# Per-row factors and second key copies of a two-layer fp32 trunk by transfers instead of transpositions

## The chip, the cores and the metric

One core of one Trainium2 chip runs the kernel. The metric is the device time of one execution in microseconds; it is the median of 3 runs. The engines are called PE (matmul), PEld (its weight load), DVE (vector), ACT (scalar), POOL (the general engine) and SP (which issues transfers); a q behind a name is the engine's sequencer.

## What is computed

A trunk of two layers on a sequence of 512 tokens of 1024 features, all in fp32. Layer 0 mixes by attention, layer 1 by a state-space scan (ssd); each is followed by a gated feed-forward part (ffn). Every part begins with an RMS norm and ends with a residual sum.

```python
for layer in range(DEPTH):
    h = rmsnorm(x, norm_mix[layer])
    if layer % 2 == 0: mix = attn_layer(h, ...)
    else:              mix = ssm_layer(h, ...)
    x = x + mix
    h = rmsnorm(x, norm_ffn[layer])
    x = x + conv_ffn(h, ...)
```

The attention layer has 8 heads B (a band of 3 chunks of 64 tokens, 2 key heads for 8 query heads, sinks) and 8 heads A (all earlier chunks, learned bias by relative position), each of 64 features, queries and keys normalised by head. A head's output is divided by its sum of exponentials:

```python
e = jnp.exp(sc - m)
p = e / (jnp.sum(e, axis=-1, keepdims=True) + jnp.exp(snk - m))
```

The ssd layer norms its gated output again in four groups of 512 features: `yg * rsqrt(mean(yg * yg) + EPS)`.

## The kernel before

Activations lie with features on the 128 partitions and the 512 tokens along the free axis, so x is eight tiles X[0] to X[7] of 128x512. A fp32 product is made of two rounded parts, hi and lo, of each operand: three matmuls (hi hi, lo hi, hi lo) in `mm3` (L154 to L159) and in `project` (L335 to L352, the input projection of attention, tokens on partitions). Weights are loaded by SP into wr, cast to wh by ACT (L150), and the rest wl is made by DVE (L151). PSUM has four banks mm for dense products, three ax for transpositions and scores, one po for head outputs.

The program sets the order within limits; a scheduler then lays each engine's instructions in one queue, which the engine goes through in order. `weave` mixes the attention units with dense products. The work the change touches:

- `Sq.rstd` (L199) makes 1/rms of each token as a 128x4 column block, tokens on partitions. The rest of the kernel needs it along the free axis, equal on all partitions: `rows` (L208 to L214) transposes four broadcast columns on PE (L211) and ACT copies the 128x512 result R to SBUF (L213). It is called seven times: for the first ffn (R is read by L627 and L637), for the ssd layer (`v` L734, the early tiles L705, `normalise` L685 to L689), four times in `gated` (R is read by `out_part`, L897, whose product is added to X in `accumulate`, L251), and for the second ffn.
- `totals` (L379 to L398), once per head pair, eight times: the reciprocals of the sums `rec` (128x8) are widened by two ACT copies (L391), transposed on PE (L395) and copied by ACT (L397) to R. `finish_pair` (L400) multiplies the head output in po by R on DVE (L402) and splits it (L405, L406).
- Scores (`scores`, L364 and L365 on PE) are evicted by DVE (L367) with the bias and go through ACT (L368); `flip` transposes them (L374, L376), `pv` multiplies with the values (L413).
- Two query heads of a pair lie on one 128-partition tile each with the other half empty, so a key head is needed in both halves. DVE writes each normalised key head twice (`twice`, L553; queries are scaled in L558), and `keys` (L321 to L333) transposes each head's 128 columns (L327), ACT makes hi (L329) and DVE lo (L330). There are ten key heads in three blocks: 2, 4 and 4.
- POOL makes the bias tiles of heads B (L451), fills a corner of each bias tile of heads A after SP has loaded it (L471), and six sums of squares (L195). Transfers from the scratch `scr` in DRAM, broadcast over the partitions, are issued by SP in the scan (L794).

Of the kernel before, what the change touches and what calls it, by code (L numbers as in the profile page):

```python
# [15 lines left out]
F32 = mybir.dt.float32  # L16
# [45 lines left out]
def trunk(ctx: ExitStack, tc: tile.TileContext, xin, w_ai, w_av, w_ao_b, w_ao_a, relp, w_dt, w_si, w_so,  # L62
# [116 lines left out]

    class Sq:  # L180
# [27 lines left out]
        def rows(self, r):  # L208
            bp = axps()
            for t in range(NT):  # L210
                nc.tensor.transpose(bp[:, t * P:(t + 1) * P], r[:, t:t + 1].to_broadcast([P, P]), ident)  # L211
            R = slot()
            nc.scalar.copy(R, bp)  # L213
            return R  # L214

# [58 lines left out]
    def attention(op, nxt, first):  # L274
# [46 lines left out]
        def keys(kn, n, g):  # L321

            hi, lo = [], []
            for h in range(n):
                tp = axps()
                for t in range(NT):
                    nc.tensor.transpose(tp[:, t * P:(t + 1) * P], kn[t][:, h * P:(h + 1) * P], ident)  # L327
                kh, kl = slot(F32R), slot(F32R)
                nc.scalar.activation(kh, tp, AF.Copy, scale=g)  # L329
                nc.vector.scalar_tensor_tensor(kl, tp, g, kh.bitcast(F32), ALU.mult, ALU.subtract)  # L330
                hi.append(kh)
                lo.append(kl)
            return hi, lo  # L333
# [45 lines left out]
        def totals(st, sink):  # L379
# [9 lines left out]
            wide = dslot()  # L389
            for i in range(2):  # L390
                nc.scalar.copy(wide.rearrange("q (p i d) -> q p i d", p=NT, i=2)[:, :, i, :],  # L391
                               rec[:, i * NT:(i + 1) * NT].unsqueeze(2).to_broadcast([P, NT, 64]))
            bp = axps()
            for p in range(NT):
                nc.tensor.transpose(bp[:, p * P:(p + 1) * P], wide[:, p * P:(p + 1) * P], ident)  # L395
            R = dslot()
            nc.scalar.copy(R, bp)  # L397
            return R  # L398

        def finish_pair(po, R):  # L400
            t = dslot()
            nc.vector.tensor_tensor(t, po, R, ALU.mult)  # L402
# [93 lines left out]
        def parts(grps):  # L496
# [9 lines left out]
            for grp, (nh, nv, turns) in enumerate(grps):  # L506
# [36 lines left out]
                twice = [None] * NT  # L543
                if nh:
                    f = head_scales(ss, nh)
                    nk = sum(n for _, name, _, n, _ in turns if name == "k")
                    nq = nh - nk
                    for t in range(NT):
                        w = raw[t][:, :nh * 64].rearrange("p (h d) -> p h d", h=nh)
                        ft = f[:, nh * t:nh * t + nh].unsqueeze(2)  # L550
                        if nk:
                            twice[t] = cslot()
                            nc.vector.tensor_tensor(  # L553
# [52 lines left out]
    def ffn(layer, op, nxt):  # L606
# [10 lines left out]
        def in_tile(f):  # L617
# [6 lines left out]
            if f == 0:  # L624
                R = op.sq.rows(r)
# [447 lines left out]
```

## Time and profile before

| | before |
|---|---|
| median of 3 runs | 1331.98 us (1331.82 to 1333.86) |
| profiled execution | 1335.82 us |
| its span on the engines | 1334.0 us |
| PE, PEld busy | 1323.0, 1076.1 us |
| DVE, ACT, POOL busy | 897.2, 592.8, 20.5 us |
| bytes moved | 130.73 MB, 98 GB/s |
| granted TensorE clock, mean | 0.997 |

Busy time of an engine is the time in which at least one of its instructions ran; matmuls overlap in the pipeline, so one's duration is longer than the distance to the next. A chain of waits is followed back from the last instruction to what released each step. A timeline line has the start, the duration, the engine, the line of the program, the operation with what it writes and reads, how many were merged into it, and in brackets how long the engine was idle before it and what ended that.

### The profile page before, as it was taken

How to read it: one execution, taken by the hardware profiler on the slowest of the kernel's cores; microseconds unless marked ns; L12 is line 12 of the kernel's file. 1: busy time of each engine (PE TensorE's matmuls, PEld its weight loads, DVE VectorE, ACT ScalarE, POOL GpSimd, SP SyncE). 2: the span in 40 equal slices, each digit the busy share in tenths (PEclk: the TensorE clock that was granted, in tenths of full speed). 3: DMA queues.
4: the chain of work that ended last, by engine and by line, in shares of the span. 5: the costliest groups of instructions: out<-in, count | busy, mean ns of one | idle time of the engine just before them, and what ended most of it. 6: DMA issues, size and time to landing. Idle time of an engine off the chain costs nothing.

```text
span 1334.0 us, 17143 instructions
## 1 busy us (share of the span) xinstructions
PE 1323.0 (99%) x6576; PEld 1076.1 (81%) x6576; DVE 897.2 (67%) x1494; ACT 592.8 (44%) x1042; POOL 20.5 (2%) x26
## 2 busy tenths in 40 slices
PE   9999999999999999999999999999999999999998
PEld 7777877788888888887788887887888888888887
DVE  5676565876446646458988896898986644664642
ACT  6576655533223323244655645546443322332321
POOL 0000000000000000020000000000000000000000
PEclk8999999999999999999999999999999999999999
DMA  7112241233332333232443333332333333333322
GB/s 238 64 52 66 74 155 44 87 99 99 103 95 95 95 96 97 85 105 62 144 127 111 103 103 96 112 99 91 95 95 95 96 99 101 100 95 95 96 72 86
DMA packets 42561, 130.73 MB, mean 98 GB/s; under 512 B 4848, under 2 KB 6128, under 8 KB 42480
## 3 DMA queue, kind: packets, MB, share of 16 engines
q1 hardware_dynamic: 41760, 129.12, 31.2%
q8 instruction: 52, 0.85, 0.3%
q10 hardware_dynamic: 720, 0.52, 0.2%
q14 instruction: 29, 0.24, 0.1%
HBM read 127.46 MB, written 2.16 MB: 97 GB/s over the span
## 4 chain that ended last, share of the span: by engine, by line
PE 93%; DVE 4%; ACT 2%; DMA 1%; issue 1%; ACTq 0%; SPq 0%; POOL 0%; POOLq 0%; DVEq 0%
PE mm L159 77%; PE mm L348 7%; PE po L413 2%; PE po L847 1%; PE ax L374 1%; DVE wl L151 1%; PE po L852 1%; PE ax L835 1%; PE ax L364 1%; ACT wh L150 1%; PE ax L365 1%; PE ax L804 1%; DMA c<-in_xin 0%; DVE d L685 0%; PE ax L201 0%
## 5 line engine op out<-in xcount | busy, mean ns | idle before, releaser
L159 PE MATMUL mm<-s,wh 128*128 128x512 f32 x3148 | 766.7, 391 | 0.7 <-DVE s L251 0.5
L159 PEld LDWEIGHTS mm<-s,wh 128*128 128x128 f32 x3148 | 585.1, 188 | 125.7 <-issue 4.6
L150 ACT CAST wh<-wr 128x1024 fp32r<-128x1024 f32 (+2 forms) x222 | 226.9, 1022 | 443.4 <-PE mm L159 404.7
L159 PE MATMUL mm<-s,wl 128*128 128x512 f32 x1574 | 398.1, 390 | 0.0
L159 PEld LDWEIGHTS mm<-s,wl 128*128 128x128 f32 x1574 | 293.8, 188 | 61.6 <-issue 1.5
L151 DVE TENSOR_TENSOR wl<-wr,wh 128x1024 fp32r<-128x1024 f32 (+2 forms) x222 | 262.8, 1184 | 41.7 <-ACT wh L150 41.1
L251 DVE TENSOR_TENSOR s<-s,mm 128x512 f32<-128x512 f32 x64 | 43.6, 687 | 125.6 <-PE mm L159 123.4
L348 PE MATMUL mm<-wh,s 128*128 128x512 f32 (+1 forms) x320 | 99.9, 389 | 3.0 <-ACT s L162 1.3
L627 DVE TENSOR_TENSOR d<-mm,s 128x512 f32<-128x512 f32 x44 | 30.4, 691 | 93.3 <-PE mm L159 90.5
L348 PEld LDWEIGHTS mm<-wh,s 128*128 128x128 f32 x320 | 58.3, 193 | 15.2 <-issue 2.4
L631 DVE SCALAR_TENSOR_TENSOR d<-d,pt,d 128x511 f32<-128x511 f32 x88 | 65.9, 749 | 3.8 <-ACT d L629 2.4
L634 ACT ACTIVATE d<-d 128x512 f32<-128x512 f32 x44 | 27.9, 634 | 86.1 <-DVE d L631 86.1
L348 PE MATMUL mm<-wl,s 128*128 128x512 f32 (+1 forms) x160 | 61.5, 384 | 0.0
L635 DVE SCALAR_TENSOR_TENSOR d<-d,d 128x512 f32<-128x512 f32 x44 | 30.5, 692 | 30.4 <-ACT d L634 30.4
L712 DVE SCALAR_TENSOR_TENSOR s<-mm,pt,s 128x511 f32<-128x511 f32 (+2 forms) x57 | 42.5, 745 | 9.6 <-ACT s L710 9.3
L813 ACT ACTIVATE c<-c,acs 128x128 f32<-128x128 f32 x128 | 41.8, 399 | 0.0
L368 ACT ACTIVATE c<-c,sm 128x256 f32<-128x256 f32 (+3 forms) x64 | 33.4, 526 | 16.5 <-DVE sm L367 15.2
L629 ACT ACTIVATE d<-d,pt 128x512 f32<-128x512 f32 x44 | 35.8, 814 | 6.0 <-DVE d L627 6.0
L637 DVE TENSOR_TENSOR d<-mm,s 128x512 f32<-128x512 f32 x44 | 30.4, 691 | 8.6 <-PE mm L159 8.5
L641 ACT CAST s<-d 128x512 fp32r<-128x512 f32 x44 | 27.4, 623 | 18.5 <-DVE d L638 18.5
L348 PEld LDWEIGHTS mm<-wl,s 128*128 128x128 f32 x160 | 31.1, 194 | 4.7 <-issue 0.3
L638 DVE TENSOR_TENSOR d<-d,d 128x512 f32<-128x512 f32 x44 | 30.5, 692 | 1.4
(155 smaller groups left out, 1026.1 us busy)
## 6 DMA issues: line engine op xcount, KB each, us to landing
wr<-in_w_fi SPq DMA_DIRECT2D x88, 512.0 KB, 3.6
wr<-in_w_si SPq DMA_DIRECT2D x40, 512.0 KB, 3.6
wr<-in_w_fo_a SPq DMA_DIRECT2D x32, 512.0 KB, 3.6
c<-scr SPq DMA_DIRECT2D x32, 256.0 KB, 4.1
wr<-in_w_so SPq DMA_DIRECT2D x16, 512.0 KB, 3.6
wr<-in_w_ai SPq DMA_DIRECT2D x12, 512.0 KB, 3.6
wr<-in_w_fo_b SPq DMA_DIRECT2D x16, 384.0 KB, 3.0
wr<-in_w_ai SPq DMA_DIRECT2D x8, 256.0 KB, 5.1
```

The lines of the kernel that those rows point to most:

```text
L150: nc.scalar.copy(h[:, cs], raw[:, cs])
L151: nc.vector.tensor_tensor(lo[:, cs], raw[:, cs], h[:, cs].bitcast(F32), ALU.subtract)
L159: nc.tensor.matmul(dst, a, b, start=start and i == 0, stop=stop and i == n - 1)
L251: nc.vector.tensor_tensor(X[m], X[m], acc, ALU.add)
L348: nc.tensor.matmul(us[t], a, b, start=k == 0 and i == 0, stop=k == KD - 1 and i == 2)
L368: nc.scalar.activation(e, e, AF.Exp, bias=st[:, n:n + 1], scale=-1.0, accum_out=st[:, 8 + n:9 + n])
L629: nc.scalar.activation(c, g, AF.Identity, bias=col(cw + 4 * f + 3), scale=col(cw + 4 * f + 2))
L631: nc.vector.scalar_tensor_tensor(c[:, sh:], g[:, :S - sh], col(cw + 4 * f + j), c[:, sh:], ALU.mult, ALU.add)
L635: nc.vector.scalar_tensor_tensor(c, th, 1.0, c, ALU.add, ALU.mult)
L638: nc.vector.tensor_tensor(u, u, c, ALU.mult)
L712: nc.vector.scalar_tensor_tensor(c[:, sh:], g[:, :S - sh], col(w0 + 3 - sh), c[:, sh:], ALU.mult, ALU.add)
L813: nc.scalar.activation(t[:, i * P:(i + 1) * P], bc[hf][:, i * P:(i + 1) * P], AF.Relu, bias=acs[:, hs + i:hs + i + 1], scale=-1.0)
```

## The change

A new function `spread` takes a block of columns (tokens on partitions) to PE for one transposition, has ACT copy the few rows that come out to SBUF, stores them from there in DRAM by a transfer that ACT issues, and loads them, broadcast over the partitions, by a transfer that POOL issues. `rows` and `totals` call it in place of their transpositions. `finish_pair` has ACT copy po to SBUF at once; DVE multiplies that copy. `keys` transposes two key heads at a time, and three half transfers issued by POOL make from each hi and lo tile the two doubled ones: first both halves of the new tile k from the second half of x, then the second half of x from its first. The scaling by 1/rms of a head is one DVE product per tile for queries and keys.

```diff
--- before.py
+++ after.py
@@ -177,6 +177,17 @@
             nc.vector.scalar_tensor_tensor(y, t, 1.5, y, ALU.add, ALU.mult)
         return y
 
+    def spread(vals, n, dst, ap):
+
+        tp = axps()[:n, :P]
+        nc.tensor.transpose(tp, vals, ident)
+        flat = sm.tile([8, P], F32, tag="flat", bufs=2, name=nm("flat"))
+        nc.scalar.copy(flat[:n, :], tp)
+        row = dp.tile([8, P], F32, name=nm("row"))
+        nc.scalar.dma_start(row[:n, :], flat[:n, :])
+        nc.gpsimd.dma_start(dst, bass.AP(tensor=row.tensor, offset=row.offset, ap=ap))
+        return dst
+
     class Sq:
 
 
@@ -206,12 +217,7 @@
             return rsqrt(v, NT)
 
         def rows(self, r):
-            bp = axps()
-            for t in range(NT):
-                nc.tensor.transpose(bp[:, t * P:(t + 1) * P], r[:, t:t + 1].to_broadcast([P, P]), ident)
-            R = slot()
-            nc.scalar.copy(R, bp)
-            return R
+            return spread(r, NT, slot(), [[0, P], [1, S]])
 
     class Operand:
 
@@ -318,18 +324,25 @@
                     res.append(q)
             return res
 
-        def keys(kn, n, g):
+        def move(dst, i, src, j):
+            nc.gpsimd.dma_start(dst[HALF[i], :].bitcast(F32), src[HALF[j], :].bitcast(F32))
+
+        def keys(kn, c0, n, g):
 
             hi, lo = [], []
-            for h in range(n):
+            for b in range(n // 2):
                 tp = axps()
                 for t in range(NT):
-                    nc.tensor.transpose(tp[:, t * P:(t + 1) * P], kn[t][:, h * P:(h + 1) * P], ident)
-                kh, kl = slot(F32R), slot(F32R)
-                nc.scalar.activation(kh, tp, AF.Copy, scale=g)
-                nc.vector.scalar_tensor_tensor(kl, tp, g, kh.bitcast(F32), ALU.mult, ALU.subtract)
-                hi.append(kh)
-                lo.append(kl)
+                    nc.tensor.transpose(tp[:, t * P:(t + 1) * P], kn[t][:, c0 + b * P:c0 + (b + 1) * P], ident)
+                h, l = slot(F32R), slot(F32R)
+                nc.scalar.activation(h, tp, AF.Copy, scale=g)
+                nc.vector.scalar_tensor_tensor(l, tp, g, h.bitcast(F32), ALU.mult, ALU.subtract)
+                for res, x in ((hi, h), (lo, l)):
+                    k = slot(F32R)
+                    move(k, 0, x, 1)
+                    move(k, 1, x, 1)
+                    move(x, 1, x, 0)
+                    res += [x, k]
             return hi, lo
 
         def project(wsrc, width, evict, mid):
@@ -386,20 +399,12 @@
                 nc.vector.tensor_tensor(st[:, 8:16], st[:, 8:16], x, ALU.add)
             rec = small(8)
             nc.vector.reciprocal(rec, st[:, 8:16])
-            wide = dslot()
-            for i in range(2):
-                nc.scalar.copy(wide.rearrange("q (p i d) -> q p i d", p=NT, i=2)[:, :, i, :],
-                               rec[:, i * NT:(i + 1) * NT].unsqueeze(2).to_broadcast([P, NT, 64]))
-            bp = axps()
-            for p in range(NT):
-                nc.tensor.transpose(bp[:, p * P:(p + 1) * P], wide[:, p * P:(p + 1) * P], ident)
-            R = dslot()
-            nc.scalar.copy(R, bp)
-            return R
+            return spread(rec, 8, dslot(), [[S, 2], [0, 64], [1, S]])
 
         def finish_pair(po, R):
             t = dslot()
-            nc.vector.tensor_tensor(t, po, R, ALU.mult)
+            nc.scalar.copy(t, po)
+            nc.vector.tensor_tensor(t, t, R, ALU.mult)
             h = slot(F32R)
             lo = slot(F32R)
             nc.scalar.copy(h, t)
@@ -540,32 +545,21 @@
                 if nv and grp == 0:
                     for t in range(NT):
                         v_copy(t, raw[t][:, nh * 64:])
-                twice = [None] * NT
                 if nh:
                     f = head_scales(ss, nh)
-                    nk = sum(n for _, name, _, n, _ in turns if name == "k")
-                    nq = nh - nk
                     for t in range(NT):
                         w = raw[t][:, :nh * 64].rearrange("p (h d) -> p h d", h=nh)
-                        ft = f[:, nh * t:nh * t + nh].unsqueeze(2)
-                        if nk:
-                            twice[t] = cslot()
-                            nc.vector.tensor_tensor(
-                                twice[t][:, :nk * P].rearrange("p (h e d) -> p h e d", h=nk, e=2),
-                                w[:, nq:, :].unsqueeze(2).to_broadcast([P, nk, 2, 64]),
-                                ft[:, nq:, :].unsqueeze(3).to_broadcast([P, nk, 2, 64]), ALU.mult)
-                        if nq:
-                            nc.vector.tensor_tensor(w[:, :nq, :], w[:, :nq, :], ft[:, :nq, :].to_broadcast([P, nq, 64]),
-                                                    ALU.mult)
-
-                def turn(raw=raw, twice=twice, vs=vs, nv=nv, turns=turns):
+                        nc.vector.tensor_tensor(w, w, f[:, nh * t:nh * t + nh].unsqueeze(2).to_broadcast([P, nh, 64]),
+                                                ALU.mult)
+
+                def turn(raw=raw, vs=vs, nv=nv, turns=turns):
                     for res, name, c0, n, g in turns:
                         if name == "v":
                             res["v"] = v_tiles(vs, nv)
                         elif name == "q":
                             res["q"] = queries(raw, c0, g)
                         else:
-                            res["k"] = keys(twice, n, g)
+                            res["k"] = keys(raw, c0, n, g)
 
                 if nh:
                     late[0] = turn
@@ -619,10 +613,8 @@
             gate = dense(w_fi[layer, f, 0])
             if f == 0:
                 op.squares()
-                r = op.sq.rstd(1024)
+                R = op.sq.rows(op.sq.rstd(1024))
             up = dense(w_fi[layer, f, 1])
-            if f == 0:
-                R = op.sq.rows(r)
             g = dslot()
             nc.vector.tensor_tensor(g, gate, R, ALU.mult)
             c = dslot()
```

The new line numbers: `spread` has its transposition on L183, the copy on L185, the store on L187, the load on L188; the moves are L328; the scores are L377 and L378.

The scheduler moves other instructions too. On DVE, at the start of the ssd layer, before (L734 makes `v`, L705 the first tile, L712 its convolution, L685 and L689 the normalised tiles):

```order
L151 TENSOR_TENSOR wl_5485<-wr_5483,wh_5484 128x1024
L734 TENSOR_TENSOR v<-mm_5197,s_5266 32x128 x4
L705 TENSOR_TENSOR d_5279<-mm_5236,s_5266 128x512
L742 TENSOR_SCALAR v<-v,pt 128x128
L712 SCALAR_TENSOR_TENSOR s_5281<-d_5279,pt,s_5281 128x511
L745 TENSOR_SCALAR ta<-ta 128x128
L712 SCALAR_TENSOR_TENSOR s_5281<-d_5279,pt,s_5281 128x510
L746 RECIPROCAL ta<-ta 128x128
L712 SCALAR_TENSOR_TENSOR s_5281<-d_5279,pt,s_5281 128x509
```

and now, where they are L726, L697, L704, and L734 the step that was L742:

```order
L151 TENSOR_TENSOR wl_5454<-wr_5452,wh_5453 128x1024
L726 TENSOR_TENSOR v<-mm_5165,s_5229 32x128 x4
L697 TENSOR_TENSOR d_5248<-mm_5204,s_5229 128x512
L734 TENSOR_SCALAR v<-v,pt 128x128
L151 TENSOR_TENSOR wl_5504<-wr_5502,wh_5503 128x1024
L704 SCALAR_TENSOR_TENSOR s_5250<-d_5248,pt,s_5250 128x511
L737 TENSOR_SCALAR ta<-ta 128x128
L704 SCALAR_TENSOR_TENSOR s_5250<-d_5248,pt,s_5250 128x510
```

The reader of R still stands right behind the split of a weight, and everything behind it in the queue follows in nearly the same order, with one split moved up into it.

On DVE, at the end of the ssd layer, before (L897 multiplies by R, here s_8414, L251 adds to X, L166 makes lo for the ffn):

```order
L151 TENSOR_TENSOR wl_8595<-wr_8593,wh_8594 128x1024
L897 TENSOR_TENSOR d_8473<-mm_8460,s_8414 128x512
L251 TENSOR_TENSOR s_1980<-s_1980,d_8473 128x512
L897 TENSOR_TENSOR d_8492<-mm_8479,s_8414 128x512
L251 TENSOR_TENSOR s_1982<-s_1982,d_8492 128x512
L151 TENSOR_TENSOR wl_8650<-wr_8648,wh_8649 128x1024
L166 SCALAR_TENSOR_TENSOR s_8477<-s_1980,pt,s_8476 128x512
L897 TENSOR_TENSOR d_8518<-mm_8505,s_8414 128x512
```

and now (L889 multiplies by R, here s_8381, L257 adds):

```order
L151 TENSOR_TENSOR wl_8568<-wr_8566,wh_8567 128x1024
L151 TENSOR_TENSOR wl_8623<-wr_8621,wh_8622 128x1024
L889 TENSOR_TENSOR d_8446<-mm_8433,s_8381 128x512
L889 TENSOR_TENSOR d_8465<-mm_8452,s_8381 128x512
L257 TENSOR_TENSOR s_1948<-s_1948,d_8446 128x512
L257 TENSOR_TENSOR s_1950<-s_1950,d_8465 128x512
L889 TENSOR_TENSOR d_8491<-mm_8478,s_8381 128x512
L889 TENSOR_TENSOR d_8511<-mm_8498,s_8381 128x512
L166 SCALAR_TENSOR_TENSOR s_8450<-s_1948,pt,s_8449 128x512
```

One more split stands ahead of the first product with R, and products and sums come in pairs; a further split that stood between them has gone behind.

On POOL, in the middle of attention, where heads B end and the keys of heads A begin, the change has (L188 loads R of a pair, L328 moves keys, L456 and L476 are the former L451 and L471):

```order
L456 TENSOR_SCALAR c_1067<-dist 128x256
L456 TENSOR_SCALAR c_1075<-dist 128x256
L188 DMA d_1111<-row_1116 128x1x512
L476 MEMSET c_1391 64x64
L188 DMA d_1321<-row_1326 128x1x512
L328 DMA s_1350<-s_1346 64x512 x2
L328 DMA s_1354<-s_1347 64x512 x2
L328 DMA s_1367<-s_1363 64x512
L328 DMA s_1346<-s_1346 64x512
L328 DMA s_1367<-s_1363 64x512
```

where before there was only

```order
L451 TENSOR_SCALAR c_1078<-dist 128x256
L451 TENSOR_SCALAR c_1086<-dist 128x256
L471 MEMSET c_1410 64x64
L471 MEMSET c_1419 64x64
L471 MEMSET c_1580 64x64
L471 MEMSET c_1589 64x64
```

The transfers now stand in the queue between products that wait for buffers and a MEMSET that waits for the load of its tile.

## Rows read from the trace of the kernel before

**Rows 1.** Page, busy time, share and instructions of each engine; the chain of waits by engine

```profile
PE 1323.0 (99%) x6576; PEld 1076.1 (81%) x6576; DVE 897.2 (67%) x1494; ACT 592.8 (44%) x1042; POOL 20.5 (2%) x26
...
PE 93%; DVE 4%; ACT 2%; DMA 1%; issue 1%; ACTq 0%; SPq 0%; POOL 0%; POOLq 0%; DVEq 0%
```

**Rows 2.** Groups by line: out<-in, shapes, count | busy us, mean ns | idle before

```profile
L327 PE MATMUL ax<-ident,c 128*128 128x128 f32 x40 | 6.2, 276 | 0.4 <-DVE c L553 0.4
...
L395 PE MATMUL ax<-ident,d 128*128 128x128 f32 x32 | 4.9, 275 | 0.5 <-DVE sm L367 0.5
...
L211 PE MATMUL ax<-ident,sm 128*128 128x128 f32 x28 | 4.3, 275 | 0.7 <-DVE sm L177 0.6
...
L213 ACT COPY s<-ax 128x512 f32<-128x512 f32 x7 | 4.1, 586 | 16.7 <-PE ax L211 16.7
```

**Rows 3.** Timeline around a head pair's sums: start, us, engine, line, operation

```profile
208.20 0.60 PE L395 MATMUL ax<-ident,d 128*128 128x128 f32 x4
...
208.56 0.36 PE L364 MATMUL ax<-s,s 128*128 128x256 f32 x1
...
209.09 0.59 ACT L397 COPY d<-ax 128x512 f32<-128x512 f32 x1
...
211.48 0.69 DVE L402 TENSOR_TENSOR d<-po,d 128x512 f32<-128x512 f32 x1 [1.02 <-ACT c L368]
```

**Rows 4.** DMA issues (KB each, median us to landing); source view of line 794

```profile
out_xt<-s SPq DMA_DIRECT2D x2, 128.0 KB, 1.7
...
scr<-ta SPq DMA_DIRECT2D x1, 64.0 KB, 4.1
...
L794 SPq DMA_DIRECT2D c<-scr x32: 319/382/461, 647.0 to 912.1; - x32
...
DMA to landing us min/median/max: 3.0/4.1/7.7
```

**Rows 5.** Timeline at the start of the ssd layer

```profile
610.12 0.58 ACT L213 COPY s<-ax 128x512 f32<-128x512 f32 x1
...
611.40 1.18 DVE L734 TENSOR_TENSOR v<-mm,s 32x128 f32<-32x128 f32 x4
...
633.06 0.19 PEld L159 LDWEIGHTS mm<-s,wh 128*128 128x128 f32 x1 [0.54 <-ACT s L688]
```

**Rows 6.** Busy time by stretch: us, then PE, PEld, DVE, ACT, POOL, PEclk

```profile
611.40:633.90 22.50, 22.39 (x100) 18.21 (x99) 21.74 (x43) 12.69 (x19) 0.00 (x0) 1.00 0.16 47
633.90:646.00 12.10, 12.10 (x61) 9.66 (x60) 11.95 (x22) 5.60 (x12) 0.00 (x0) 1.00 0.43 130
...
950.00:965.00 15.00, 15.00 (x70) 12.43 (x69) 14.11 (x21) 6.68 (x9) 0.00 (x0) 1.00 0.48 150
```

**Rows 7.** Timeline at the end of the ssd layer

```profile
951.21 0.59 ACT L213 COPY s<-ax 128x512 f32<-128x512 f32 x1 [1.50 <-PE ax L211]
...
951.83 0.69 DVE L897 TENSOR_TENSOR d<-mm,s 128x512 f32<-128x512 f32 x1
...
970.71 0.69 DVE L251 TENSOR_TENSOR s<-s,d 128x512 f32<-128x512 f32 x1
...
972.31 0.19 PEld L159 LDWEIGHTS mm<-s,wh 128*128 128x128 f32 x1 [0.22 <-ACT s L228]
```

**Rows 8.** Timeline at the start of the second ffn

```profile
986.02 0.69 DVE L627 TENSOR_TENSOR d<-mm,s 128x512 f32<-128x512 f32 x1 [1.42 <-ACT s L213]
```

**Rows 9.** Timeline around the first scores of attention

```profile
47.82 1.41 DVE L330 SCALAR_TENSOR_TENSOR s<-ax,pt,s 128x512 fp32r<-128x512 f32 x2
...
50.05 0.33 PE L364 MATMUL ax<-s,s 128*128 128x128 f32 x1
```

**Rows 10.** Timeline of POOL; source view of line 451 (duration ns min/median/max)

```profile
173.07 0.14 POOL L471 MEMSET c<- 64x64 f32 x1 [25.99 <-DMA c<-in_relp]
...
L451 POOL TENSOR_SCALAR c<-dist x8: 842/852/2226, 16.8 to 99.8; 128x256 f32<-128x256 f32 x8
```

**Rows 11.** Busy time by stretch, the first 14.3 us

```profile
0.00:14.30 14.30, 11.05 (x35) 8.77 (x36) 7.34 (x17) 9.52 (x16) 0.20 (x4) 0.78 0.86 280
```

## The prediction

> **What bounds the kernel now.** I read the page's table of engines and its chain of waits first. PE is busy for 1323.0 of 1334.0 us and the chain runs through it for 93% of its length [rows 1]; so the kernel gets shorter only where PE gets less to do, and longer wherever PE is made to stand. Then I read the timelines of the places where the change puts a transfer between a short PE step and the DVE operation that reads its result, and the busy time of DVE there: whether DVE can make up for a wait decides each price. The profiled execution took 1335.8 us (span 1334.0); the median of the runs is 1332.0, 3.8 lower. I make the sum against the first and take it over to the second.
>
> **What leaves PE.** The groups of transposes [rows 2]: L211 28, L395 32, L327 40 instructions. After the change 7, 8 and 20 are left, 65 fewer. Their 275 ns is not what one costs, as they are pipelined: four of L395 begin at 208.20 and the next PE instruction begins at 208.56 [rows 3], 0.09 us each. 65 x 0.09 = **-5.9 us**, all of it on the chain. What goes on ACT (L213, L391, half of L329) and DVE (L553, half of L330) is hidden, as both engines have idle time between 40 and 245 us, where all but L213 stand.
>
> **What a row R costs in time.** Before: R is on SBUF 0.59 us after its four transposes (L397 at 209.09, [rows 3]). Afterwards it goes out of SBUF by one transfer and comes back by another that waits for it. For the first the nearest rows are a store of 128 KB, 1.7 us, and the store of 64 KB to scratch, 4.1; for the second the broadcast loads of 256 KB from scratch, 3.0 at the least, 4.1 median, 7.7 at most [rows 4]. Those are issued by SP; no row shows a load that POOL issues. Ends: 1.7 + 3.0 = 4.7 and 4.1 + 4.1 = 8.2 us. I call this delay L and take L = 6.5, the middle: the first transfer is much smaller than either row, the second has a POOL issue ahead of it that no row prices. (The Trainium skill, "DMA: Bandwidth & Descriptors", section on the anatomy of a DMA on the gpsimd path, gives a transfer issued by GpSimd a fixed 2.0 us and its bytes at 436 GB/s: an estimate of 2.6 us for 256 KB, and with 2.1 for the first, L near 4.7. No run here shows it; it is the quick rival below.)
>
> **Start of the ssd layer.** The DVE operations of the first tiles all read R. L213 ends at 610.70, and the first reader L734 begins at 611.40, after a wl split [rows 5]. In the new order that reader still stands right behind the split, and all of DVE's work behind it: R lands at 610.5 + L, so DVE stands L - 0.9 us longer. It has 21.74 of 22.50 us busy up to 633.9, and 11.95 of 12.10 in the next stretch [rows 6], so it cannot catch up. PE meets this at the first tile that needs normalised operands, where it already waited 0.54 us for L688, the cast behind the last of DVE's eight L685 [rows 5]: no slack. I take off 0.76 us of DVE's idle time, 0.7 for one operation of 0.69 us that the new order puts behind the last L685, and 0.7 for three matmuls that it puts ahead on PE. Price L - 3.0: **1.7 to 5.2, taken 3.5.**
>
> **End of the ssd layer.** The last R (four transposes, copy L213 at 951.21) is read by L897 at 951.83; eight such products and eight L251 sums follow, and the last sum begins at 970.71 and ends at 971.4. The first tile of ffn needs the operand made from it, and PE waited 0.22 us for it at 972.31 [rows 7]: no slack again. DVE was busy 14.11 of the 15.00 us from 950 on [rows 6]. The new order puts one more wl split ahead of the wait and others behind the last sum, so from R on there are 17 operations of about 0.64 us, 6 of 0.67 and one split of 1.15, that is 16.1 us. R at 951.3 + L gives the sum's end at 967.4 + L, against 971.4. Price L - 4.0 and a little for PSUM banks that come free late: **0.8 to 4.3, taken 2.8.**
>
> **Starts of ffn.** The ffn's first product L627 began at 986.02, 1.42 us of idle behind L213 [rows 8]; its bank is needed again two tiles later, at about 993 here and 12 us later in the first ffn. R lands 990 to 994. **0 to 1.7, taken 0.5.** The three other group rows (gated, groups 0 to 2) are read many us later: nothing; what hides them is the scan, and without it each would cost L.
>
> **Attention, eight R of head pairs.** L402 read po right behind its R; it came 1.7 to 5.8 us after the transposes, 3.3 in the one shown (208.20 to 211.48, [rows 3]). Now ACT copies po out (one more copy of 0.59, beside PE) and the product waits L. po comes free earlier, which PE did not wait for. But the product stands in DVE's queue ahead of score evictions and of weight splits; they stand with it up to 5 us, eight times. PE goes on until its next score finds all three banks uncollected: 19 to 38 PE instructions in the new order, 3 to 6 us. So a block passes on 0 to 1.5 us: **0 to 12, taken 3.5**, nearer to nothing, as dense matmuls lie between.
>
> **Second copies of keys.** Each pair's hi and lo get three half transfers, the third behind the other two: two in series, 3.4 (2 x 1.7) to 8.2 us (2 x 4.1) [rows 4]. First block: lo parts are made from 47.82 on, the first done at 48.5, and PE read them from 50.05 on [rows 9]. The new order puts 13 more dense matmuls of 0.23 us ahead of the first hi score and 18 ahead of the first lo score: 52.7 and 53.9, against 51.9 to 56.7 for lo. 0 to 2.8, taken 1. The two blocks of heads A have twelve transfers each in one queue and 33 dense matmuls (7.5 us) of cover: 0 to 3 each, taken 1. **Together 0 to 9, taken 3.** (The Trainium skill, "DMA: Bandwidth & Descriptors", rules for kernel authors, says that two transfers to disjoint partition halves serialize and that one of 128 partitions serves better; that speaks for the upper end. No run here shows it.)
>
> **POOL's queue.** It held 8 bias products, 8 MEMSETs and 6 sums; now 45 transfers stand between them, in order. A MEMSET waits for its relp load, up to 25.99 us [rows 10]. In the new order the fourth pair's R stands behind a MEMSET; its load was moved ahead on SP, and I charge nothing. If it isn't early enough, that R and the keys behind it are late by whole transfers.
>
> **Sum:** -5.9 + 3.5 + 2.8 + 0.5 + 3.5 + 3 = +7.4, 1343.2 for the profiled execution and **1339.5 us** on the scale of the median. No change means within 0.2%, 2.7 us, about what a measurement of this kernel can tell.
>
> **The rivals.**
> *Quick transfers, faster.* The two ends of the ssd layer cost together 2L - 7.0. At L = 4.0 they cost 1.0, and if DVE's blocks in attention and the keys stay under their covers (1 us in all), the sum is -3.9: 1328. It decides from L below 4.5 us. For it: the order was laid with the keys' first use put off by 18 matmuls. Against: DVE is full at both ends of ssd [rows 6, 7]. With L = 4.7, and 1.5 each for attention and keys, it comes to -0.5: 1331.5, no change. A chance of 0.19 for faster, 0.13 for no change.
> *POOL late, much slower.* If a POOL issue takes 1 to 2 us instead of the 0.38 us of SP's [rows 4], twelve key transfers take 12 to 24 us instead of 7.5, and L is 8. A bias product took 842 ns at the least and 2226 at most [rows 10], so something holds POOL up beside a busy DVE. Ssd 9.0, attention 8, keys 9, ffn 1.5: +21.6, 1353.6; a R behind a MEMSET adds up to 8. (The Trainium skill, "GPSIMD Engine Reference", specifications, has GpSimd share its SBUF interface with VectorE, in contention with DVE operations of two SBUF inputs; the spread of L451 agrees.) 0.2.
> *The clock.* PE's granted clock was 0.78 as a mean of the first 14.3 us, where PE waited for its first loads [rows 11]. Should a pause in attention bring the lower level back, 1.2 in place of 2.4 GHz, a dense matmul of 0.22 us (100 in 22.39, [rows 6]) would take as much again: 2.2 us on top for every ten. It is in the upper end, 0.03 together with what else may go wrong.
> The forecast itself, 1335 to 1346: 0.45, which with the two cases above it makes 0.68 for slower.
>
> **The range.** 1327 to 1353 leaves out the cases of no cost at all and the worst of POOL's queue. Faster 0.19, same 0.13, slower 0.68.
>
> **What would show it.** PE busy time 5 to 6 us shorter, idle time of PE 13 us longer. At the start of ssd the first product of the dt values begins 4 to 7 us after the single transposition's copy, and PE's wait for L688's successor is 3 to 5 us instead of 0.54. At its end PE waits 2 to 4 us for the first ffn operand. DVE's longest waits name the broadcast transfer. Wrong would be: L under 4.5 us, or a DVE that catches up before PE needs it, or the first scores waiting over 5 us for keys.

## The result, and the profile after

The changed kernel takes 1399.56 us (median of 4 runs, 1395.98 to 1403.92) against 1332.92 for the one before beside it: ratio 1.0501, 95% interval [1.0488, 1.0514]. It is 66.6 us slower; the prediction had 1339.5 and a range up to 1353. The page of the profile after, its engines and its chain ([rows 1] before):

```profile
PE 1335.6 (96%) x6511; PEld 1083.8 (78%) x6511; DVE 888.7 (64%) x1481; ACT 584.9 (42%) x1029; POOL 46.0 (3%) x71
...
PE 85%; DMA 8%; DVE 4%; issue 2%; ACT 1%; POOL 0%; ACTq 0%; SPq 0%; POOLq 0%; DVEq 0%
```

The 65 transposes are gone, yet PE is busy 12.6 us longer, and idle for 58.6 us of its span instead of 11.0. Where that happened is read from the transpositions for R, which stand at the same place in both programs: 255.88, 608.97, 950.58 and 984.75 before, 308.67, 661.11, 1008.33 and 1045.85 after.

```profile
255.88 0.62 PE L211 MATMUL ax<-ident,sm 128*128 128x128 f32 x4 [0.18 <-DVE sm L177]
...
608.97 0.60 PE L211 MATMUL ax<-ident,sm 128*128 128x128 f32 x4
...
950.58 0.60 PE L211 MATMUL ax<-ident,sm 128*128 128x128 f32 x4
...
984.75 0.62 PE L211 MATMUL ax<-ident,sm 128*128 128x128 f32 x4
```

```profile
308.67 0.27 PE L183 MATMUL ax<-ident,sm 128*4 128x128 f32 x1 [0.18 <-DVE sm L177]
...
661.11 0.27 PE L183 MATMUL ax<-ident,sm 128*4 128x128 f32 x1
...
1008.33 0.27 PE L183 MATMUL ax<-ident,sm 128*4 128x128 f32 x1
...
1045.85 0.27 PE L183 MATMUL ax<-ident,sm 128*4 128x128 f32 x1
```

| stage | before | after | difference |
|---|---|---|---|
| to the first ffn (attention) | 255.88 | 308.67 | +52.8 |
| first ffn | 353.09 | 352.44 | -0.7 |
| ssd to its last R | 341.61 | 347.22 | +5.6 |
| last R to the second ffn's R | 34.17 | 37.52 | +3.4 |
| second ffn | 349.25 | 348.35 | -0.9 |

The differences add up to 60.2 us, the distance of the two profiled executions (1395.98 and 1335.82 us); the medians lie 66.6 apart. So attention holds nearly nine tenths of what the profiles show. Busy time by stretch (columns as in [rows 6]: PE, PEld, DVE, ACT, POOL, then the granted clock), attention before and after:

```profile
40.00:255.30 215.30, 212.11 (x1255) 164.55 (x1254) 141.05 (x348) 132.02 (x328) 7.35 (x14) 1.00 0.25 78
```

```profile
40.00:308.00 268.00, 222.56 (x1204) 172.55 (x1203) 132.94 (x330) 126.40 (x312) 29.43 (x53) 0.89 0.29 85
```

PE's idle time there went from 3.2 to 45.4 us. Its busy time rose by 10.5 us with 51 recorded instructions fewer, because the granted clock fell to a mean of 0.89: if a stretch has either the full clock or half of it, 0.11 x 2 x 268 = 59 us ran at half.

One of the eight head pairs, as the timeline of the changed kernel has it:

```profile
69.89 0.27 PE L183 MATMUL ax<-ident,sm 128*8 128x128 f32 x1
...
70.48 0.53 ACTq L187 DMA_DIRECT2D row<-flat  x1
...
71.99 0.87 POOL L188 DMA_DIRECT2D d<-row  x1 [7.08 <-DMA row<-flat]
...
77.28 1.06 PE L361 MATMUL mm<-wh,s 128*128 128x512 f32 x2
78.13 0.63 PE L361 MATMUL mm<-wl,s 128*128 128x512 f32 x1
80.23 0.69 DVE L407 TENSOR_TENSOR d<-d,d 128x512 f32<-128x512 f32 x1 [5.55 <-DMA d<-row]
80.95 0.62 ACT L410 CAST s<-d 128x512 fp32r<-128x512 f32 x1 [4.62 <-DVE d L407]
81.48 0.58 ACT L527 COPY d<-mm 128x512 f32<-128x512 f32 x1
...
82.11 0.79 PE L361 MATMUL mm<-wh,s 128*128 128x512 f32 x1 [3.35 <-ACT d L527]
```

The store took 1.5 us to POOL's issue, the load another 8.2 to DVE's product. DVE stood for 5.55 us. ACT stood behind it for 4.62, since the cast L410 waits for the product, and behind the cast stood L527, which copies a finished bank out. PE waited 3.35 us for that bank. Over the eight pairs it was 9.2 to 11.9 us from the end of the copy to `flat` to the product, and DVE stood 2.9 to 8.0 us at each. The two dense matmuls from 77.28 took 0.43 us each, not 0.22: the clock had fallen already, behind shorter waits of PE in the same pair (0.41, 0.54 and 1.02 us up to 75.42).

### The profile page after: what moved, and what is told of

The parts are those of the page before. It is cut to its first block, busy times and chain, and to the rows that moved or that the text cites. A ratio compares the mean times of both kernels' runs of the same rounds, so it can differ in the third digit from the quotient of the medians.

```text
span 1394.2 us, 17097 instructions
## 1 busy us (share of the span) xinstructions
PE 1335.6 (96%) x6511; PEld 1083.8 (78%) x6511; DVE 888.7 (64%) x1481; ACT 584.9 (42%) x1029; POOL 46.0 (3%) x71
## 4 chain that ended last, share of the span: by engine, by line
PE 85%; DMA 8%; DVE 4%; issue 2%; ACT 1%; POOL 0%; ACTq 0%; SPq 0%; POOLq 0%; DVEq 0%
PE mm L159 73%; PE mm L361 5%; DMA d<-row 3%; DMA s<-s 2%; PE po L839 1%; DMA row<-flat 1%; PE ax L387 1%; PE po L418 1%; DMA s<-row 1%; PE po L844 1%; PE ax L827 1%; DVE wl L151 1%; PE ax L377 1%; PE ax L796 1%; PE ax L378 0%
## 5 line engine op out<-in xcount | busy, mean ns | idle before, releaser
L257 DVE TENSOR_TENSOR s<-s,mm 128x512 f32<-128x512 f32 x64 | 43.8, 686 | 131.5 <-PE mm L159 127.6
L361 PE MATMUL mm<-wh,s 128*128 128x512 f32 (+1 forms) x320 | 105.8, 404 | 5.8 <-ACT d L527 4.4
L361 PEld LDWEIGHTS mm<-wh,s 128*128 128x128 f32 x320 | 61.6, 203 | 18.9 <-ACT d L527 5.3
L704 DVE SCALAR_TENSOR_TENSOR s<-mm,pt,s 128x511 f32<-128x511 f32 (+2 forms) x57 | 42.4, 744 | 9.7 <-ACT s L702 9.3
L387 PE MATMUL ax<-ident,c 128*128 128x128 f32 x136 | 26.0, 300 | 12.3 <-DVE sm L380 11.7
L633 ACT CAST s<-d 128x512 fp32r<-128x512 f32 x44 | 27.3, 621 | 17.7 <-DVE d L630 17.7
```

What stands on the lines that cost most here:

```text
L257: nc.vector.tensor_tensor(X[m], X[m], acc, ALU.add)
L361: nc.tensor.matmul(us[t], a, b, start=k == 0 and i == 0, stop=k == KD - 1 and i == 2)
L387: nc.tensor.transpose(tp[:, b * P:(b + 1) * P], e[:, b * P:(b + 1) * P], ident)
L704: nc.vector.scalar_tensor_tensor(c[:, sh:], g[:, :S - sh], col(w0 + 3 - sh), c[:, sh:], ALU.mult, ALU.add)
```

## The experiments

Times are medians; "before" is the kernel before, measured beside each run on the same chip; the brackets hold the 95% interval of the ratio. Profiles show one execution of each kernel.

**Parts alone.** `t_only` changes `totals` and `finish_pair`, `k_only` the keys and their scaling, `r_only` `rows` with the order in ffn; each is the hunks of the diff for that part.

t_only: 

> The kernel before with the sums of head pairs and the copied-out head outputs alone changed. Theory W (DVE stands at each product with R for the two transfers, PE runs dry behind it and then gets the lower clock): the profile of the changed kernel has 42.6 us of DVE waits at the eight products, five to eight stretches at half the clock, and 46 us of the chain on the loads of R, so this part alone gives most of the attention's 53 us: +30 to +42 us against before. Theory K (the key moves are what costs): below +15 us. Theory M (the parts only cost together, since one's pauses use up the other's cover): below +20 us here and below +8 us for keys alone.

1377.83 against 1332.99 us, ratio 1.0338 [1.0308, 1.0368].

k_only: 

> The kernel before with the second copies of keys alone moved by POOL's transfers. Theory W: the moves are second in the chain (25 us of its attention part), so +8 to +20 us, with PE waits for the moved keys of 2 to 6 us per block at most. Theory K: over +30 us. Theory M: below +8 us.

1345.22 against 1332.99, ratio 1.0093 [1.0064, 1.0122].

r_only: 

> The kernel before with the 1/rms rows alone changed. From the changed kernel, where the transposition of R at the start of ssd, at its end and at the second ffn lie 52.1, 57.8 and 61.1 us later than before and the end 60.2: the ssd layer's two R cost 5.6 and 3.4 us together with little given back: +7 to +10 us under every theory, and no wait in attention. If the first ffn's R costs too, 1 to 2 us more.

1340.83 against 1332.99, ratio 1.0068 [1.0045, 1.0091].

44.8 + 12.2 + 7.8 = 64.8 of 66.6 us: the parts add up, and the sums of head pairs are two thirds. Theory W holds for where the cost lies, though 44.8 is a little above its range; M and K fall.

**Is it the wait?** Edit on t_only:

```diff
-            nc.vector.tensor_tensor(t, t, R, ALU.mult)
+            t4 = t.rearrange("p (a b) -> p a b", a=NT)
+            nc.vector.tensor_tensor(t4, t4, ones.unsqueeze(1).to_broadcast([P, NT, P]), ALU.mult)
```

t_still: 

> As the sums alone, but the product of the copied head output reads a tile of ones that lies in SBUF from the start instead of R; the transfers are still made and R is not used (the division by the sums is left out). Theory W: nothing stands for R, PE has 24 transposes less and no pause: -2 to +4 us against before, and the clock stays at the upper level. A theory T in which the transfers themselves or their issue on POOL and ACT slow the other engines: most of the cost of the sums alone stays, over +15 us.

1328.71 against 1332.99, ratio 0.9972 [0.996, 0.9984]. All transfers are made and the kernel is 4.3 us faster than before: so all that the sums cost comes from the wait for R. That is more than was expected. The 24 transposes are worth some 2.2 us of the 4.3 by the prediction's 0.09 us each; what gives the rest I didn't test.

**How the load is made.** Edit on t_only, in `spread`:

```diff
-        nc.gpsimd.dma_start(dst, bass.AP(tensor=row.tensor, offset=row.offset, ap=ap))
+        for i in range(2):
+            nc.gpsimd.dma_start(dst[i * 64:(i + 1) * 64, :],
+                                bass.AP(tensor=row.tensor, offset=row.offset + i * S, ap=[[0, 64], [1, S]]))
```

t_two: 

> As the sums alone, but R comes back by two loads, each of one row of 512 broadcast over 64 partitions, in place of one load with a pattern of two rows. In the trace the one load moved 448 packets of 8 bytes beside 64 of 4 KB and took 7.0 to 8.5 us to land, the loads of the 1/rms rows only packets of 4 KB and 3.2 to 5.0. Theory P (the pattern makes the load slow): landing falls to 3 to 5 us, DVE's waits at the eight products from 44.5 to 10 to 25 us, and the time to +8 to +25 us against before (sums alone: +44.8). Theory Q (POOL or the queue makes it slow): landing stays above 6 us and the time above +38 us.

1335.01 against 1332.38, ratio 1.0017 [1.0003, 1.003]. Nearly the whole 44.8 us goes with one load made into two, more than theory P expected. The source view of the load, in t_only and in t_two (who waited: us in total, times; then landing):

```profile
  DVE d L405: 44.5, 8
...
DMA to landing us min/median/max: 7.0/7.3/8.5
```

```profile
  DVE d L407: 8.3, 4
...
DMA to landing us min/median/max: 2.7/2.9/5.4
```

I read this as the 8-byte packets' doing; the next run shows that it wasn't. Edit on t_only: the load's `nc.gpsimd` becomes `nc.sync`.

t_sp: 

> As the sums alone, the same load pattern of two rows, but issued by SP instead of POOL. If any issuer makes 8-byte packets of this pattern: 448 of them per load again, landing above 6 us, +35 us or more. If only POOL's queue does: packets of 2 or 4 KB, landing 3 to 4.5 us, and +0 to +15 us, where SP's weight loads behind the waiting load may add some.

1377.64 against 1333.65, ratio 1.0333 [1.0314, 1.0351]. SP's queue carried no 8-byte packets of it, 128 of 2 KB per load, and DVE waited as before (source view):

```profile
L188 SPq DMA_DIRECT2D d<-row x8: 512/517/628, 63.4 to 258.7; - x8
...
  DVE d L405: 42.5, 8
```

Neither POOL nor the packets' size is the cause. In t_sp undisturbed packets took 84 ns each, and a load's 128 were spread over 5.2 us at the least: 128 x 84 / 5200 = two at a time. Two is the outermost dimension of the load's pattern `[[S, 2], [0, 64], [1, S]]`. This number was raised by writing each reciprocal two or four times beside itself before the transposition (on t_only, here for 4; n is the number of rows that come out):

```diff
-            rec = small(8)
-            nc.vector.reciprocal(rec, st[:, 8:16])
+            rec = small(16)
+            nc.vector.reciprocal(rec.rearrange("q (i r p) -> q i r p", i=2, r=2),
+                                 st[:, 8:16].rearrange("q (i p) -> q i p", i=2).unsqueeze(2).to_broadcast([P, 2, 2, NT]))
...
-            return spread(rec, 8, dslot(), [[S, 2], [0, 64], [1, S]])
+            return spread(rec, 16, dslot(), [[S, 4], [0, 32], [1, S]])
```

t_k4: 

> As the sums alone, one load from POOL, but the reciprocals go to DRAM in two copies, so that the load's outermost dimension is 4 instead of 2. In the sums alone the packets of a load ran two at a time (64 big ones of 159 ns in 5.4 us), from SP's queue too (128 of 84 ns in 5.2 us). Theory O (the outermost dimension is the number of DMA engines that share a load, whoever issues it): packets in 2.7 us, landing 4.3 to 5.2 us instead of 7.3, DVE's waits at the products 15 to 30 us instead of 44.5, +8 to +25 us against before instead of +44.8. If a pattern of this kind is slow for another reason (its mere number of dimensions): landing stays above 6.5 us, +35 us or more.

1351.24 against 1334.15, ratio 1.013 [1.01, 1.0159]. Its source view, and that of t_k8 behind it:

```profile
  DVE d L406: 24.0, 6
...
DMA to landing us min/median/max: 4.6/4.9/5.9
```

t_k8: 

> The same with four copies, an outermost dimension of 8. Theory O: packets in 1.4 to 1.7 us, landing 2.9 to 3.8 us, DVE's waits 5 to 15 us, 0 to +8 us against before, close to the two loads (+2.3). If the pattern is slow for another reason: as with 4.

1339.97 against 1334.15, ratio 1.0052 [1.0032, 1.0072].

```profile
  DVE d L406: 15.0, 6
...
DMA to landing us min/median/max: 3.4/3.5/3.6
```

| load of R | packets lie over | landing, median | DVE waits | clock, 40 to 300 us | against before |
|---|---|---|---|---|---|
| outermost 2 | 5.3 to 6.8 us | 7.3 us | 44.5 us | 0.91 | +44.8 us |
| outermost 4 | 2.8 to 3.7 | 4.9 | 24.0 | 0.96 | +17.1 |
| outermost 8 | 1.6 to 2.1 | 3.5 | 15.0 | 0.99 | +5.8 |
| two loads of 64 rows | 1.3 to 4.0 | 2.9 | 8.3 | 0.98 | +2.6 |

All but the last column are from the profiled execution; that of t_two took 1339.3 us, 4.3 above its median. The loads bring the same bytes by the same queue, and 64 packets of 159 ns over 5.3, 2.8 and 1.6 us at the least make 1.9, 3.6 and 6.4 at a time, with 2, 4 and 8 as the outermost dimension: theory O holds. The 8-byte packets fell along with it, from 448 to 192 and 64 per load; that they are not the cause is t_sp's to say, which had none and was as slow. Dimensions 4 and 8 were not run from SP. The Trainium skill says it outright ("DMA: Bandwidth & Descriptors", rules for kernel authors): an outermost dimension of c below 16 confines the whole transfer to at most c DMA engines. The runs agree at 2, 4 and 8. The same section of the Trainium skill has the rule that the prediction weighed for the keys, that two transfers to partition halves serialize and gain nothing, as both run on all engines anyway. It doesn't fit this load, whose packets ran two at a time: here the halves took 42 us off.

**How the wait reaches PE.** Edit on t_only: the cast to hi in `finish_pair` becomes `nc.gpsimd.tensor_copy(h, t)`.

t_act: 

> As the sums alone with the slow load, but the cast to hi behind the product runs on POOL, so that ACT no longer stands behind the product and only DVE does. Sums alone: +44.8, with PE waiting both for scores that DVE evicts late and for banks that ACT copies out late. If ACT's stand is the larger way by which the wait reaches PE: +5 to +25. If DVE's is: +30 to +45.

1377.42 against 1333.65, ratio 1.0331 [1.0312, 1.035]: no gain that could be told, so DVE's stand alone is enough (PE now waited 4.3 us for POOL's cast once, which may hide a small one). PE's waits between 40 and 300 us, first t_only's largest, then t_act's:

```profile
PE ax L385 <- DVE sm L378: 15.7, 4, 5.2
```

```profile
PE ax L385 <- DVE sm L378: 20.1, 6, 5.5
```

Edit on t_only: product, cast and rest all on `nc.gpsimd`.

t_pool: 

> As the sums alone, but the product with R, the cast to hi and the rest lo all run on POOL, so that neither DVE nor ACT stands for the load; the load is as slow as before. Theory W (what costs is that DVE and ACT stand in order behind the product): no lower clock in attention, no pause over 2 us, -5 to +3 us against before. Rival (the head outputs themselves come too late for their consumers, or POOL's work beside DVE slows it): +5 us or more, with PE waiting for the parts of the head outputs.

1352.8 against 1332.38, ratio 1.0153 [1.0124, 1.0183]. Less than half is left, but the rival came true: PE waited 6.9 us for POOL's cast, and up to 6.4 for a score evicted late, as POOL's other work now stood behind the product (DVE's score evictions waited 10.7 us for POOL's MEMSETs L474). PE's two largest waits between 40 and 300 us (in total, times, longest):

```profile
PE ax L385 <- DVE sm L378: 8.5, 2, 6.4
PE mm L159 <- POOL s L408: 6.9, 1, 6.9
```

So that DVE and ACT stand is a large part of the cost, but how large this run doesn't show.

**The clock's share.** Edit on t_only: `warm(16)` behind `spread` in `totals`, 16 matmuls of `ones`.

t_warm: 

> As the sums alone, with 16 matmuls of ones by ones, read by nobody, behind each of the eight transpositions: they give PE some 3.4 us of work at full clock each, 27 us in all. The sums alone added 32 us of PE idle time and 11 us of PE busy time, in spite of 24 transposes less, with 48 us at half the clock. Theory C (a quarter to a third of the cost is the lower clock, which comes where PE has paused): the pauses are filled, the stretches at half clock go or shrink below 20 us, and although PE does 27 us more, the time is 5 to 14 us below the sums alone (+31 to +40 against before). Theory I (the pauses alone count, the clock nothing): the work goes into the pauses at best, 0 to +5 us against the sums alone (+45 to +50).

1376.89 against 1332.38, ratio 1.0334 [1.0304, 1.0364], between the two expectations. The page, and the added matmuls of one pair up to the next instruction:

```profile
PE 1350.8 (98%) x6808; PEld 1105.1 (80%) x6808; DVE 897.3 (65%) x1494; ACT 589.0 (43%) x1034; POOL 27.0 (2%) x34
```

```profile
61.94 3.73 PE L131 MATMUL ax<-ones 128*128 128x128 f32 x32
65.43 0.36 PE L377 MATMUL ax<-s,s 128*128 128x256 f32 x1
```

The trace has 32 for the 16 of one pair; 32 in 3.49 us make 256 in 27.9. t_only had PE busy for 1333.9 us; 16.9 more for 27.9 of added work means that 11 us of slow matmuls went, and the mean clock rose from 0.981 to 0.994. So of the 44.8 us some 11, by this estimate, were the clock and the rest idle time. PE's idle time fell by 17.7 us, as much as its busy time rose, so the total stayed: the clock's 11 us were won, but the added work did not fit into the pauses.

**Keys without their series.** k_eng writes all four halves of a pair's two tiles from PSUM on ACT and DVE. k_two writes each half where it belongs and moves one half per tile:

```diff
-                    move(k, 0, x, 1)
-                    move(k, 1, x, 1)
-                    move(x, 1, x, 0)
+                    nc.scalar.activation(h[own, :], tp[own, :], AF.Copy, scale=g[own, :])
+                    move(h, 1 - i, h, i)
```

k_eng: 

> The kernel before with two key heads to a transposition, as in the change, but both halves of each key tile written straight from PSUM by ACT and DVE (eight half-tile operations per pair instead of four whole ones), with no transfer. Keys by transfers cost +12.2 us. Theory W (the two transfers in series are what costs): -3 to +2 us against before, as 20 transposes (1.8 us) go and ACT and DVE have room. Rival (the later keys cost whatever makes them, since a pair's keys now come out of one bank): +4 us or more.

1331.84 against 1332.38, ratio 0.9991 [0.998, 1.0003]: without transfers the 12.2 us are gone.

k_two: 

> The kernel before with keys by pairs, but ACT and DVE write each half where it belongs in its own tile, and one move per tile fills the other half: 20 moves of which none waits for another, in place of 30 with every third behind two. Keys as in the change cost +12.2 us, keys without any move -0.5 us. If the third move behind the other two is the cost: +1 to +5 us. If the moves' number or POOL's issue is: +8 us or more.

1330.96 against 1333.23, ratio 0.9983 [0.9973, 0.9993]: faster than before, which I had not expected. PE's first scores in k_only, with hi and with lo:

```profile
52.46 0.42 PE L371 MATMUL ax<-s,s 128*128 128x128 f32 x2 [1.40 <-DMA s<-s]
...
56.75 0.69 PE L372 MATMUL ax<-s,s 128*128 128x128 f32 x2 [2.65 <-DMA s<-s]
```

In k_two no engine waits for a move, and a move lands in 2.4 us instead of 3.2 (KB each, medians; first k_only, then k_two):

```profile
s<-s POOLq DMA_DIRECT2D x30, 128.0 KB, 3.2
```

```profile
s<-s POOLq DMA_DIRECT2D x20, 128.0 KB, 2.4
```

Number and series of the moves were changed together; which counts more stays open.

**Combinations.** a_two is the whole change with two loads; r_hid spreads the five rows at ffn and in the groups 0 to 2 only; best is k_eng with r_hid, best2 k_two with r_hid, best3 is best2 with the sums in two loads.

a_two: 

> The whole change, but each R of a head pair comes back by two loads of one row each. The parts alone added up to the whole (44.8 + 12.2 + 7.8 = 64.8 of 66.6 us), and two loads took 42.5 us off the sums' part. If the load's pattern is the step that failed, the whole costs +20 to +27 us against before (12.2 + 7.8 + 2.3 = 22.3). If the parts share their waits after all: over +32 us.

1359.35 against 1333.23, ratio 1.0196 [1.0178, 1.0215]: +26.1, near the upper end of the first range, so the load's pattern made most of the whole change's cost too.

r_hid: 

> The kernel before with five of the seven 1/rms rows by transfers (both ffn, the gated groups 0 to 2), the two at the start and at the end of the ssd layer as before. If the rows' +7.8 us lie at those two alone, as the starts of the stages show: -2 to +1 us (15 transposes less, 1.4 us). If the others cost too: +3 us or more.

1332.16 against 1333.23, ratio 0.9996 [0.9987, 1.0005]: no cost of the five is seen, so the rows' cost is at the two ends of ssd. Its 1.1 us by medians are within the interval of no change.

best: 

> Keys by pairs with both halves written from PSUM (no transfers; -0.5 us alone) and the five hidden 1/rms rows by transfers; sums of head pairs as before. If both keep what they save: -1 to -3 us against before, 1329.5 to 1331.5. If one meets the other's cover: 0 to +2 us.

1330.57 against 1333.23, ratio 0.9981 [0.9972, 0.999].

best2: 

> Keys by pairs with one move per tile (-2.3 us alone) and the five hidden 1/rms rows by transfers (-1.1 us alone), sums of head pairs as before. If the two keep their gains: -2.5 to -4.5 us against before. If not: about -2.3 or less.

1327.97 against 1333.65, ratio 0.9961 [0.9948, 0.9973]. It is 5.7 us faster than the kernel before, more than was expected. Its page:

```profile
PE 1314.2 (99%) x6541; PEld 1068.8 (81%) x6541; DVE 892.9 (67%) x1486; ACT 591.4 (45%) x1042; POOL 33.7 (3%) x51
```

best3: 

> As the one before with the sums of head pairs by transfers too, in two loads (+2.3 us alone, of which a stretch at half the clock was part; without any wait for R, -4.3). If the waits for R stay above their cover: 0 to +3 us against before. If this order hides them: -4 to -7 us.

1339.36 against 1333.65, ratio 1.0051 [1.0036, 1.0067]: above the +3 that was expected at most. Even with the fast load the sums are better left on PE, 11 us between best2 and best3.

## Why the prediction was wrong, point by point

**The step that failed** is "Attention, eight R of head pairs: 0 to 12, taken 3.5". Measured: 44.8, with the 24 transposes already taken off. Three things in it were wrong. No one of them makes the 44.8: with the waits of DVE as t_only had them (2.2 to 8.9 us) and the prediction's cover of 3 to 6 for each, the term would have come to some 6 to 22 us, an estimate.

*One L for all R.* The prediction priced every load by the broadcasts of [rows 4], 3.0 to 4.1 us. For the rows of the norms that was right: from the flat copy to the reader 5.8 us at the start of ssd, 7.6 at its end. For the head pairs the copy ends at 70.45 and the product begins at 80.23: 9.8, and 9.2 to 11.9 over the eight, all outside 4.7 to 8.2. The diff showed the difference beforehand, an outermost dimension of 2 for this load and of 128 for the other. Where the head pairs' load was as quick as the prediction took it, the term held: in t_k8 the product came 5.4 to 8.1 us behind the copy, and the sums cost +5.8, or 8.0 with the transposes' 2.2 added back.

*The cover.* 3 to 6 us of PE work was taken as hiding a stand of up to 5. But DVE's waits per pair were 2.9 to 8.0 us, and PE was idle 42 us more in the stage. Measured from t_still, the same program without the wait (-4.3), 8.3, 15.0, 24.0 and 44.5 us of DVE waits cost 6.9, 10.1, 21.4 and 49.1 us: 0.7 to 1.1 us for each (1.4 for the first, if t_two's profiled execution is taken in place of its median), so there was hardly any cover. What PE waits for in this stage, by t_only's list, stands in DVE's queue: score evictions (L378), splits of transposed keys and queries (L341, L327) and sums into X (L262). ACT's own stand at the cast was missing too; t_act says that without it the time is the same.

*The clock* stood among the rivals with 0.03. It was some 11 us of the sums, and part of the rest; that each new wait could bring it back was not in the term.

**Second copies of keys**, 3 taken, 0 to 9: mis-sized. 12.2 measured, 14 with the 20 transposes' 1.8 added back. The series of two was named and its upper end was the right one: the first block's lo keys were ready at 56.7, the end of the 51.9 to 56.7, where 1 us was taken. PE's waits for moved keys in k_only come to 4.6 us in all; the clock fell behind them in the first block (0.50 from 56.7 to 60.1 us), and another 3.3 us PE waited for a sum into X (L251) that stood for a load of x. The term had neither of these, and how the rest of the 12.2 us is made up stays open.

**Ssd, start**, 3.5 taken: L 5.8, price by the formula 2.8. DVE did not catch up, as forecast, but PE's wait for the cast L680 (the former L688) was 1.7 us where 3 to 5 were named. The stage took 5.6 us more, and 0.8 more than that without the nine transposes saved in the groups. Two waits are seen, and the clock behind them (0.50 from 687.5 to 694.3 us); the bank that waits for L697 and the clock the formula didn't have:

```profile
662.26 0.25 ACT L185 COPY flat<-ax 4x128 f32<-4x128 f32 x1
...
668.29 1.19 DVE L726 TENSOR_TENSOR v<-mm,s 32x128 f32<-32x128 f32 x4 [4.67 <-DMA s<-row]
...
685.80 1.11 PE L159 MATMUL mm<-s,wh 128*128 128x512 f32 x2 [1.74 <-ACT s L680]
...
688.88 1.65 PE L159 MATMUL mm<-s,wh 128*128 128x512 f32 x3 [1.32 <-DVE d L697]
```

**Ssd, end**: 2.8 taken, 3.4 measured, and luck had a part in it. The first product with R came at 1016.49, 7.6 us behind the copy. PE waited 1.7 us for a bank, which the prediction had only as "a little", and 0.38 us for the first operand of the ffn, where 2 to 4 were named:

```profile
1008.64 0.26 ACT L185 COPY flat<-ax 4x128 f32<-4x128 f32 x1 [2.86 <-PE ax L183]
...
1016.49 1.29 DVE L889 TENSOR_TENSOR d<-mm,s 128x512 f32<-128x512 f32 x2 [3.94 <-DMA s<-row]
...
1017.33 1.17 PE L159 MATMUL mm<-s,wh 128*128 128x512 f32 x4 [1.69 <-DVE d L889]
...
1030.26 2.82 PEld L159 LDWEIGHTS mm<-s,wh 128*128 128x128 f32 x13 [0.38 <-ACT s L234]
```

**Starts of ffn**, 0.5 taken: the stages came out 0.7 and 0.9 shorter, though PE waited 1.7 us once. **Transposes**, -5.9: not measured by themselves. r_hid gains 1.1 us for 15 of them, within its noise; t_still gains 4.3 for 24, where more than the transposes was changed. **POOL's queue**: a POOL issue took 0.5 to 0.9 us, less than the rival's 1 to 2; the late load was not POOL's doing (t_sp). The 7.5 us beside which that rival sets its twelve issues is the keys' cover; twelve of SP's 0.38 us are 4.6. **PE's totals**: 5 to 6 us less busy and 13 more idle were named; it was 12.6 more busy and 47.6 more idle, by the slow clock and the waits in attention. The direction was right, the rival that came nearest (1353.6) named the wrong cause, POOL.

## What to carry to other kernels

Before a transfer takes the place of an engine's work on a wait's path, look at its pattern's outermost dimension: here it set how many of its packets ran at a time, and rows of another transfer of the same size didn't price it. Where PE is full and an in-order engine collects its results, a first price for each us that this engine stands is one us of the kernel, lower clock included, as it was here (0.7 to 1.4). What paid is work taken off the bound engine whose result nobody waits for: here keys by one move per tile and the rows that are read late.

## What the runs showed that I had not expected

A load of 256 KB from POOL's queue landed in 3.5 us with an outermost dimension of 8, 4.9 with 4 and 7.3 with 2; from SP's queue, with 2, its packets lay over as long a time. Transfers that nobody waits for cost nothing that was seen: t_still moved the same bytes and was 4.3 us faster than the kernel before. And 27.9 us of added matmuls left the time of t_only where it was (1376.9 and 1377.8 us), since they ran in part in pauses and kept the clock up.
